# Hybrid attention and expert block: where the experts' collected rows are summed, gated and added

## The chip, the cores and the metric

The kernel runs on one core of one Trainium2 chip. The time is the device time of one launch in microseconds; lower is better. Engines are called as the profile calls them: PE (matmuls), PEld (its weight loads), DVE (VectorE), ACT (ScalarE), POOL (GpSimd) and SP (SyncE, which here only issues DMAs). Each engine works through its own list of instructions in order, so an instruction that waits holds up all that stand behind it on that engine.

## The reference

Two layers run over 256 latent tokens and 256 context tokens of width 1024, in float32. A layer is a modulated norm, a projection, two branches (neighbourhood attention, and a long convolution), a gated merge into `x`, and then a mixture of 32 experts of which every token takes two. The last layer computes only the latent tokens to the end; of the context it needs keys and values.

```python
def _layer(x, xc, c, c_ctx, last, ...):
    h = _rms(x, norm_mix) * (1.0 + sc1) + sh1          # hc for the context in the same way
    q, k, v, hy, gates = _project(h, w_in, q_norm, k_norm)
    ...
    x = x + g1 * _merge(attn, hyena, gates, w_br_a, w_br_b, w_out)
    h2 = _rms(x, norm_ffn) * (1.0 + sc2) + sh2
    x = x + g2 * _hier_moe(h2, ...)                    # top-1 group, two experts of it
    if last:
        return x, xc
    ...
    xc = xc + g2c * _hier_moe(h2c, ...)
    return x, xc
```

An expert computes `(silu(h2 @ w1) * (h2 @ w3) * weight) @ w2`; a token's two results are added, multiplied by the gate `g2` (one row of 1024 for the latent tokens, another for the context) and added to `x`.

## The kernel before, in words

Rows of tokens are held in tiles of 128: in layer one tiles 0 and 1 are latent and 2 and 3 context (`nt` is 4, `full` is true), in layer two there are only 0 and 1. `xm[0]` holds rows 0 and 1 side by side, `xm[1]` rows 2 and 3.

The expert stage (`moe`, `first_round`) goes through eight groups `q` of four experts, two pairs of experts each; below, pair p is experts 2p and 2p+1, so group 6 is pairs 12 and 13 and group 7 is pairs 14 and 15. Of each expert three blocks of 1 MiB are loaded by SP (`fetch`, line 1391) into a ring of SBUF buffers: two for the first product, one for the second. A block is loaded as soon as the block that had its buffer has been used. For a pair PE runs the first product (`w13`, L1411, 32 matmuls), `hidden` makes the gate product out of it (ACT `sl`, DVE `hd` at L1365, two transposes at L1368, ACT `hdT`), and PE runs the second product (`w2`, L1426, 16 matmuls). The second product of a pair waits for its gate product; the first product of the next pair stands around it.

Groups 0 to 5 write their results to DRAM, in rows by token (`scatter`, L1292, into `ybuf`, two rows for a token). Groups 6 and 7 don't: their results stay in SBUF and are brought to the tokens' rows by matmuls with a one-hot matrix (`add`, L1456), and `residual` multiplies by the gate and adds to `x`. What groups 0 to 5 wrote is read back by `collect(i)`: POOL issues two loads of 512 KiB for row tile i (L1306), and the `add` that it returns sums them, multiplies by `g2` and adds to `x`: three DVE instructions over 128x1024 for each of the tiles, all on DVE. In layer one `collect(0)` and `collect(1)` are called in group 6, `collect(2)` and `collect(3)` in group 7 after the first gate product; in layer two `collect(0)` in group 6 and `collect(1)` in group 7. `collect(0)` also loads `g2` (L394, SP). In layer one rows 0 and 2 go to the buffer s21, all others to the two rotating buffers `t4`.

The code's order is not the order of the engines' lists. A planner sorts the instructions by its own estimates of times: an instruction goes on its engine's list when, by the estimate, its inputs are there. It can so put an instruction that waits for a DMA ahead of one that comes before it in the code. `issue_after(ins)` forbids that for one instruction: what is inside stands behind `ins` on the same engine's list, and that is all it does.

After group 7 a block that runs only when an expert has over 64 tokens is passed by a branch (L1350); nothing moves across it. Layer two begins with `head([0, 1])`: norm (`xn`, L457), transposes (L461), scaled and split to `hT`. The projection that follows runs 12 times 24 matmuls (`proj_T`, L239 to L241), each with a weight tile `wsp` that ACT and DVE split in advance; `head([2, 3])` for the context stands after the sixth of them. It calls `residual(i, half, None)`, which adds what groups 6 and 7 gave the context's rows (kept in `rest`, buffer s21) to `x`. Layer two's expert ring has 16 buffers, s15 among them.

## Time and profile before

| what | value |
|---|---|
| time, median of 3 runs | 1447.03 us (1446.01 to 1447.13) |
| profiled execution | 1441.07 us |
| its span | 1439.3 us |
| PE busy | 1281.0 us (89%) |
| DVE busy | 660.3 us (46%) |
| ACT busy | 455.8 us (32%) |
| POOL busy | 211.0 us (15%) |
| moved by DMA | 373.04 MB, mean 259 GB/s |
| expert stage of layer one | about 603 to 885 us |
| expert stage of layer two | about 1180 us to the end |

The profile is one execution. Its times count from the span's start. In the timeline a row gives the start, the time taken, the engine, the line, the operation, what it writes and reads, and in brackets how long the engine had been idle before it and whose end released it. A span's busy share does not tell what bounds a stage; that is read from the waits of the stage.

### The profile page before, as it was taken

What the parts mean: (1) busy time and instruction counts of PE and PEld (TensorE: products, weight loads), DVE (VectorE), ACT (ScalarE), POOL (GpSimd) and SP (SyncE); (2) the same over time, 40 slices, a digit from 0 to 9 for tenths busy, and PEclk for the clock granted to TensorE, in tenths of its full rate; (3) what the DMA queues carried; (4) which work ended last, traced back from release to release, by engine and by line L of the source; (5) the groups of instructions that cost most, each with busy time, mean ns of one, the idle gap of its engine ahead of it and who ended that gap; (6) DMA issues with size and microseconds to landing.
All of it is one profiled execution on the core that took longest, in us unless ns stands there. A gap on an engine that the chain in (4) does not pass through costs nothing. (4 is left out here: it accounts for less than half of the span.)

```text
span 1439.3 us, 18183 instructions
## 1 busy us (share of the span) xinstructions
PE 1281.0 (89%) x7071; PEld 831.1 (58%) x7071; DVE 660.3 (46%) x1361; ACT 455.8 (32%) x884; POOL 211.0 (15%) x175
## 2 busy tenths in 40 slices
PE   5999999999999999599888397999899969998776
PEld 2555777886578887344333134899779943443222
DVE  4654366676677666601000137865774760100014
ACT  3433223337632133222211014533574522221101
POOL 2021033361000000211110000032500021110000
PEclk9999999999999999699999699999999979999989
DMA  9744625455177762799999963325326749999991
GB/s 377 282 166 185 230 90 190 159 219 215 59 262 274 288 241 98 278 408 420 419 420 422 403 274 137 129 106 211 136 94 219 259 161 380 418 419 420 422 407 69
DMA packets 65691, 373.04 MB, mean 259 GB/s; under 512 B 11994, under 2 KB 13338, under 8 KB 26048
## 3 DMA queue, kind: packets, MB, share of 16 engines
q1 hardware_dynamic: 54368, 347.67, 61.9%
q0 software_dynamic: 10368, 21.02, 4.1%
q10 hardware_dynamic: 864, 3.15, 0.5%
q8 instruction: 57, 0.93, 0.3%
q14 instruction: 34, 0.28, 0.1%
HBM read 362.06 MB, written 27.53 MB: 271 GB/s over the span
## 5 line engine op out<-in xcount | busy, mean ns | idle before, releaser
L1411 PE MATMUL pW<-we,xT 128*64 128x512 f32 x1024 | 263.0, 605 | 8.5 <-DMA we<-in_wexp_dram 8.4
L1411 PEld LDWEIGHTS pW<-we,xT 128*64 128x64 f32 x1024 | 82.3, 138 | 149.8 <-issue 131.7
L239 PE MATMUL pA<-hT,wsp 128*128 128x512 f32 (+1 forms) x448 | 156.3, 349 | 4.0 <-ACT hf L223 4.0
L1365 DVE SCALAR_TENSOR_TENSOR hd<-sl,cws,pW 128x256 f32<-128x256 f32 x32 | 15.3, 480 | 305.9 <-ACT sl L223 305.9
L241 PE MATMUL pA<-hT,wsp 128*128 128x512 f32 (+1 forms) x448 | 154.4, 345 | 1.1 <-DVE wsp L220 1.1
L240 PE MATMUL pA<-hT,wsp 128*128 128x512 f32 (+1 forms) x448 | 154.0, 344 | 0.0
L220 DVE TENSOR_TENSOR wsp<-win,wsp 128x1024 fp32r<-128x1024 f32 x80 | 102.1, 1281 | 105.8 <-ACT wsp L223 105.6
L1426 PE MATMUL pW<-we,hdT 128*64 128x512 f32 x512 | 142.0, 621 | 4.9 <-ACT hdT L223 4.7
L223 ACT ACTIVATE wsp<-win 128x1024 fp32r<-128x1024 f32 x80 | 84.1, 1057 | 141.9 <-PE pA L241 137.2
L240 PE MATMUL pA<-wsp,hT 128*128 128x256 f32 x352 | 99.9, 284 | 2.6 <-DVE wsp L220 2.6
L239 PE MATMUL pA<-wsp,hT 128*128 128x256 f32 x352 | 100.2, 285 | 0.7 <-ACT vv L223 0.7
L241 PE MATMUL pA<-wsp,hT 128*128 128x256 f32 x352 | 99.7, 283 | 0.0
L239 PEld LDWEIGHTS pA<-hT,wsp 128*128 128x128 f32 x448 | 86.2, 192 | 21.6 <-issue 8.0
L240 PEld LDWEIGHTS pA<-hT,wsp 128*128 128x128 f32 x448 | 86.1, 192 | 13.7 <-issue 6.1
L241 PEld LDWEIGHTS pA<-hT,wsp 128*128 128x128 f32 x448 | 85.9, 192 | 11.1 <-issue 1.8
L1426 PEld LDWEIGHTS pW<-we,hdT 128*64 128x64 f32 x512 | 48.6, 141 | 73.3 <-issue 59.2
L223 ACT ACTIVATE Y<-pW 128x512 f32<-128x512 f32 (+1 forms) x64 | 38.2, 597 | 137.0 <-PE pW L1426 134.7
L223 ACT ACTIVATE sl<-pW 128x256 f32<-128x256 f32 x32 | 12.3, 383 | 218.7 <-PE pW L1411 218.7
L248 POOL TENSOR_TENSOR rs<-rsq,mh 128x1 f32<-128x1 f32 x14 | 8.4, 601 | 424.9 <-DVE rsq L247 414.0
L239 PEld LDWEIGHTS pA<-wsp,hT 128*128 128x128 f32 x352 | 67.3, 191 | 5.3 <-issue 2.5
L240 PEld LDWEIGHTS pA<-wsp,hT 128*128 128x128 f32 x352 | 67.4, 191 | 3.4 <-DVE wsp L220 3.2
L241 PEld LDWEIGHTS pA<-wsp,hT 128*128 128x128 f32 x352 | 67.4, 191 | 0.2
(301 smaller groups left out, 2324.4 us busy)
## 6 DMA issues: line engine op xcount, KB each, us to landing
we<-in_wexp_dram SPq DMA_DIRECT2D x190, 1024.0 KB
win<-in_win_dram SPq DMA_DIRECT2D x40, 1024.0 KB
ada<-in_ada_dram SPq DMA_DIRECT2D x32, 1024.0 KB
ada<-in_adaj_dram SPq DMA_DIRECT2D x16, 1024.0 KB
wbr<-in_wbr_dram SPq DMA_DIRECT2D x8, 1024.0 KB
wout<-in_wout_dram SPq DMA_DIRECT2D x8, 1024.0 KB
ybuf<-zero SPq DMA_DIRECT2D x12, 512.0 KB
bc<-modd SPq DMA_DIRECT2D x12, 512.0 KB
```

Source lines behind the costliest of these rows:

```text
L220: (eng or self.nc.vector).tensor_tensor(out=out, in0=a, in1=b, op=op)
L223: self.nc.scalar.activation(out, in_, func, **kw)
L239: self.nc.tensor.matmul(out, lh, rh, start=start, stop=False)
L240: self.nc.tensor.matmul(out, lh, rl, start=False, stop=False)
L241: self.nc.tensor.matmul(out, ll, rh, start=False, stop=stop)
L248: nc.gpsimd.tensor_tensor(out=out, in0=t, in1=self.mh[:, : shape[1]], op=ALU.pow)
L1365: nc.vector.scalar_tensor_tensor(out=hd, in0=sl, scalar=cws, in1=pa[:, 256:512], op0=ALU.mult, op1=ALU.mult)
L1411: nc.tensor.matmul(pa[64 * e : 64 * e + 64, :], xT[:, kc, cs], wt[(2 * p + e, kc // 4)][:, kc % 4, :], start=kc == 0, stop=kc == KC - 1)
L1426: nc.tensor.matmul(py[64 * e : 64 * e + 64, :], hdT[:, fc, 64 * e : 64 * e + 64], wt[(2 * p + e, 2)][:, fc, hs], start=fc == 0, stop=fc == 1)
```

## The change

The sum and the gate product move from DVE to POOL for all rows, and the two row tiles of latent tokens are collected together in group 6 in both layers; in layer two the first of them gets the buffer s15, for which the expert ring gives that buffer up for its last 16 blocks. What is left on DVE for the latent tokens is one addition to `x` for each tile, ordered behind the last gate product (`last_hd`, pair 15). The context's rows of layer one are no longer collected in the expert stage: their four loads, and one of the context's gate row (`gc`, SP), stand behind the branch; POOL sums and gates them in the head of layer two, and DVE adds them to `x` in `head([2, 3])`, ahead of `residual`.

```diff
--- before.py
+++ after.py
@@ -443,6 +443,7 @@
             i0, n = tiles[0], len(tiles)
             for i in tiles:
                 if not full and i > 1:
+                    self.tt(xs[1][:, i % 2, :], xs[1][:, i % 2, :], self.crows[i - 2][0], ALU.add)
                     for half in range(2):
                         self.residual(i, half, None)
                 x_ = xs[i // 2][:, i % 2, :]
@@ -473,6 +474,13 @@
             head([0, 1, 2, 3])
         else:
             head([0, 1])
+            y0, y1, gc = self.crows[0]
+            first = nc.gpsimd.tensor_tensor(out=y0, in0=y0, in1=y1, op=ALU.add).ins
+            with self.tc.issue_after(first):
+                self.tt(y0, y0, gc, ALU.mult, nc.gpsimd)
+                y0, y1, gc = self.crows[1]
+                self.tt(y0, y0, y1, ALU.add, nc.gpsimd)
+                self.tt(y0, y0, gc, ALU.mult, nc.gpsimd)
         if full:
             self.filter(0, 0, (17, 19), 12, "B", "B", "C")
             self.ft = self.fin[2]
@@ -1297,19 +1305,19 @@
             nonlocal g2
             if i == 0:
                 g2 = self.bcast(l, 3, 0 if full else 20, ns)
-            if full and i % 2 == 0:
-                yr = self.S(21, [P, 2, D], name="yr")
+                yr = self.S(21 if full else 15, [P, 2, D], name="yr")
                 yt = [yr[:, 0, :], yr[:, 1, :]]
             else:
                 yt = [self.T4([P, D], name="yt") for _ in range(2)]
             for k in range(2):
                 nc.gpsimd.dma_start(yt[k], ybuf[(k * nt + i) * P : (k * nt + i) * P + P, :])
+            self.tt(yt[0], yt[0], yt[1], ALU.add, nc.gpsimd)
+            self.tt(yt[0], yt[0], g2[:, 0, :], ALU.mult, nc.gpsimd)
 
             def add():
-                x_ = xm[i // 2][:, i % 2, :]
-                self.tt(yt[0], yt[0], yt[1], ALU.add)
-                self.tt(yt[0], yt[0], g2[:, i // 2, :], ALU.mult)
-                self.tt(x_, x_, yt[0], ALU.add)
+                x_ = xm[0][:, i, :]
+                with self.tc.issue_after(self.last_hd):
+                    self.tt(x_, x_, yt[0], ALU.add)
             return add
 
         ssn = [self.st([P, 2], "ss", 4) for _ in range(nt if full else 0)]
@@ -1355,6 +1363,16 @@
                     nc.sync.dma_start(self.out[0, i * P : i * P + P, hs], xm[0][:, i, hs])
         self.xres, self.rsn = xm, rsn
         self.residual = residual
+        if full:
+
+            gc = self.T4([P, D], name="gc")
+            nc.sync.dma_start(gc, self.modd[l, 3, 1:2, :].partition_broadcast(P)[:, 0, :])
+            self.crows = []
+            for i in (2, 3):
+                yr = self.S((17, 19)[i - 2], [P, 2, D], name="yc")
+                for k in range(2):
+                    nc.gpsimd.dma_start(yr[:, k, :], ybuf[(k * nt + i) * P : (k * nt + i) * P + P, :])
+                self.crows.append((yr[:, 0, :], yr[:, 1, :], gc))
 
     def hidden(self, pa, cws):
 
@@ -1362,7 +1380,8 @@
         sl = self.TH([P, 256], name="sl")
         self.act(sl, pa[:, 0:256], AF.Silu)
         hd = self.TH([P, 256], name="hd")
-        nc.vector.scalar_tensor_tensor(out=hd, in0=sl, scalar=cws, in1=pa[:, 256:512], op0=ALU.mult, op1=ALU.mult)
+        self.last_hd = nc.vector.scalar_tensor_tensor(out=hd, in0=sl, scalar=cws, in1=pa[:, 256:512],
+                                                      op0=ALU.mult, op1=ALU.mult).ins
         ptt = self.ps("X", [P, 2, P])
         for fc in range(2):
             nc.tensor.transpose(ptt[:, fc, :], hd[:, fc * P : fc * P + P], self.ident)
@@ -1385,7 +1404,8 @@
         else:
             order = [(e, k) for e in range(NEXP) for k in range(3)]
             order[84:] = [(e, k) for e in range(28, 32) for k in range(2)] + [(e, 2) for e in range(28, 32)]
-            seq = [15, 18, 11, 13, 16, 21, 2, 3, 17, 19, 4, 5, 6, 7, 8, 9] * 6
+            seq = [15, 18, 11, 13, 16, 21, 2, 3, 17, 19, 4, 5, 6, 7, 8, 9] * 5
+            seq += seq[1:16] + [18]
         prev = [max([-1] + [m for m in range(n) if seq[m] == seq[n]]) for n in range(96)]
 
         def fetch():
@@ -1478,16 +1498,13 @@
                 spread(q)
             hdT = self.hidden(w13(2 * q, z["xT"], fill), z["cw"][:, 0:1])
             if q == 7:
-                for u in adds:
-                    u()
-                adds = [collect(i) for i in range(nt // 2, nt)]
                 self.banks["X"] = [7]
             if q > 5:
                 z["Y"].append(self.S(ys[0][q % 2], [P, 2, D], F32R, name="Y"))
                 outs.append(to_parts(z["Y"][0]))
             fill = w2(2 * q, hdT, outs[0])
             if q == 6:
-                adds = [collect(i) for i in range(nt // 2)]
+                adds = [collect(i) for i in range(2)]
             if q == 7:
                 fill += [lambda x=x: open_(*x) for x in units]
             hdT = self.hidden(w13(2 * q + 1, z["xT"], fill), z["cw"][:, 1:2])
```

## Rows read from the trace of the kernel before

**Rows 1.** The page: its first line, and PE's share of the span.
```profile
span 1439.3 us, 18183 instructions
...
PE 1281.0 (89%) x7071; PEld 831.1 (58%) x7071; DVE 660.3 (46%) x1361; ACT 455.8 (32%) x884; POOL 211.0 (15%) x175
```
**Rows 2.** PE's waits, 600 to 880 us: total us, times, longest us.
```profile
PE pX L1368 <- DVE hd L1365: 31.2, 7, 22.8
```
**Rows 3.** PE's waits, 1180 us to the end.
```profile
PE pX L1368 <- DVE hd L1365: 17.8, 5, 13.8
```
**Rows 4.** Timeline around pair 12's gate product, layer one.
```profile
790.17 0.38 ACT L223 ACTIVATE sl<-pW 128x256 f32<-128x256 f32 x1 [6.55 <-PE pW L1411]
...
792.63 1.07 POOL L1306 DMA_DIRECT2D yt<-ybuf  x2
...
811.30 1.23 DVE L220 TENSOR_TENSOR yt<-yt,yt 128x1024 f32<-128x1024 f32 x1 [6.29 <-DMA yt<-ybuf]
812.44 0.48 DVE L1365 SCALAR_TENSOR_TENSOR hd<-sl,cws,pW 128x256 f32<-128x256 f32 x1
...
812.97 0.69 PE L1368 MATMUL pX<-cst,hd 128*128 128x128 f32 x2 [22.84 <-DVE hd L1365]
```
**Rows 5.** Timeline around pair 12's gate product, layer two.
```profile
1362.33 0.38 ACT L223 ACTIVATE sl<-pW 128x256 f32<-128x256 f32 x1 [7.95 <-PE pW L1411]
1374.43 1.23 DVE L220 TENSOR_TENSOR yt<-yt,yt 128x1024 f32<-128x1024 f32 x1 [26.72 <-DMA yt<-ybuf]
1375.57 0.48 DVE L1365 SCALAR_TENSOR_TENSOR hd<-sl,cws,pW 128x256 f32<-128x256 f32 x1
...
1376.11 0.69 PE L1368 MATMUL pX<-cst,hd 128*128 128x128 f32 x2 [13.81 <-DVE hd L1365]
```
**Rows 6.** Both stretches by windows: busy by engine, then PEclk, DMA share, GB/s.
```profile
790.00:813.00 23.00, 0.16 (x2) 0.03 (x1) 2.84 (x3) 0.38 (x1) 2.39 (x5) 0.60 1.01 418
...
1362.00:1376.00 14.00, 0.29 (x1) 0.00 (x0) 1.57 (x2) 0.38 (x1) 1.21 (x3) 0.59 1.02 421
```
**Rows 7.** Timeline, pair 15 of layer one.
```profile
864.60 0.38 ACT L223 ACTIVATE sl<-pW 128x256 f32<-128x256 f32 x1 [9.98 <-PE pW L1411]
...
867.42 0.47 DVE L1365 SCALAR_TENSOR_TENSOR hd<-sl,cws,pW 128x256 f32<-128x256 f32 x1
...
868.86 5.37 PE L1426 MATMUL pW<-we,hdT 128*64 128x512 f32 x16 [0.47 <-ACT hdT L223]
```
**Rows 8.** Windows where the weights' stream ends, both layers.
```profile
844.00:846.00 2.00, 2.00 (x12) 0.64 (x10) 0.00 (x0) 0.00 (x0) 0.00 (x0) 1.00 0.04 16
846.00:848.00 2.00, 2.00 (x10) 0.56 (x6) 0.00 (x0) 0.00 (x0) 0.00 (x0) 1.00 0.00 0
...
1410.00:1412.00 2.00, 2.00 (x10) 0.63 (x10) 1.79 (x2) 0.35 (x1) 0.00 (x0) 1.00 0.05 19
```
**Rows 9.** Timeline, PE in pairs 14 and 15 of layer two.
```profile
1401.42 7.08 PE L1411 MATMUL pW<-we,xT 128*64 128x512 f32 x30
...
1423.50 3.65 PE L1426 MATMUL pW<-we,hdT 128*64 128x512 f32 x16
```
**Rows 10.** Timeline, PE in the head of layer two: first projection, context's transposes.
```profile
893.28 0.51 PE L239 MATMUL pA<-hT,wsp 128*128 128x256 f32 x1 [2.57 <-ACT hf L223]
...
913.35 0.60 PE L461 MATMUL pA<-cst,xn 128*128 128x128 f32 x4
```
**Rows 11.** Timeline, collecting row tile 2 in layer one.
```profile
853.01 1.05 POOL L1306 DMA_DIRECT2D yr<-ybuf  x2 [39.66 <-DVE x L220]
...
860.36 1.22 DVE L220 TENSOR_TENSOR yr<-yr 128x1024 f32<-128x1024 f32 x1 [5.02 <-DMA yr<-ybuf]
```
**Rows 12.** Groups of POOL by form: count | busy us, mean ns | idle before.
```profile
L220 POOL TENSOR_TENSOR Yj<-Yj,t 128x512 f32<-128x512 f32 x24 | 32.3, 1357 | 141.6 <-DVE t L220 121.4 <-ACT hf L223 20.2
...
L220 POOL TENSOR_TENSOR wf<-Yj 128x512 f32<-128x512 f32 x12 | 20.9, 1740 | 0.9
```
**Rows 13.** Timeline, SP in layer two's projection: issues and the waits between them.
```profile
907.07 32.19 SPq L212 DMA_DIRECT2D win<-in_win_dram  x5
```

## The prediction

> **What bounds the kernel now.** I read the page first, then PE's waits in each of the two expert stages, then the timeline around the longest wait, then the windows of the stretch with the DMA share, and last the place where the weights' stream ends. PE is busy for 1281.0 us of the span of 1439.3 us [rows 1], so what can be won is idle time of PE at places where PE is last.
>
> PE's longest single waits in both expert stages are of one kind: the transposes of a gate product wait for DVE's `hd`, once for 22.8 us in layer one [rows 2] and once for 13.8 us in layer two [rows 3]. The timeline shows why. In layer one ACT has pair 12's `sl` at 790.17 + 0.38 = 790.55 us, but `hd` starts at 812.44, because the planner put the sum of the collected rows `yt` ahead of it, and that sum starts only at 811.30, when its load has landed. The load was issued at 792.63 [rows 4]. In layer two `sl` is there at 1362.71, the sum starts at 1374.43, `hd` at 1375.57 [rows 5]. During both waits the DMA engines are full, 418 and 421 GB/s [rows 6]: the collected rows come late because the weights' stream fills the same engines, and while PE waits the stream runs ahead of it. PE's granted clock falls to a mean of 0.60 and 0.59 there, which lies between full speed and the low level of 1.2 GHz, so PE also starts again slowly.
>
> The gain has a second limit. The stream of weights cannot end earlier merely because DVE no longer waits. In layer one packets still move in the window 844 to 846 us and none in the next; in layer two a few still move between 1410 and 1412 us [rows 8]. The last product of a layer needs the last blocks.
>
> **Part 1: the sums and gates of the latent rows leave DVE (layer one).** `hd` of pair 12 can start at about 790.6 instead of 812.44, 21.9 us earlier. At pair 15 six DVE instructions for the context's rows stand ahead of `hd` too: `sl` is there at 864.98, `hd` starts at 867.42, 2.4 us late [rows 7]. Both go. By PE alone the second product of pair 15, which starts at 868.86 [rows 7], would start 21.9 + 2.4 = 24.3 us earlier, at 844.6. By the stream it can start when the last block is in, at about 846 [rows 8]. The later one counts: 846, a gain of 22.9 us. That product took 5.37 us against 3.65 us for the same 16 matmuls in layer two [rows 7, 9]; if PE comes to it at full clock another 1.7 us fall away, if PE has idled for the last blocks they don't. I take 23 us; the bounds are 18 (both products of pair 15 at the low clock, some 5 us) and 28 (the stream ends earlier, and PE alone counts: 24.3 + 1.7, and some 2 us of low clock behind the wait that go too).
>
> **Part 2: the same in layer two.** `hd` of pair 12 starts at about 1362.75 instead of 1375.57, 12.8 us earlier. By PE alone the last second product starts at 1423.50 - 12.8 = 1410.7 [rows 9]. The stream gets 0.5 MiB more ahead of its end (the second load of row tile 1 now goes with the other three), 0.52 MB at 421 GB/s or 1.25 us, so it ends at about 1412.5 instead of 1411.3 [rows 6, 8]. The blocks on the way also hold PE, which works in order. An estimate from these rows: 9.5 MiB stand behind the first block of expert 29 in the stream, 2.5 us each, so that block lands at 1412.5 - 23.7 = 1388.8. Behind it PE has half of pair 13's second product (half of 3.65), some ten one-hot products (7.08 / 30 = 0.24 us each), 7.1 for pair 14's first product, and the 15.0 us that lie between the end of that product and the start of the last one, 1408.50 to 1423.50 [rows 9]: 1388.8 + 1.8 + 2.4 + 7.1 + 15.0 = 1415.1. So the product starts at 1412.5 to 1415 and the gain is 8.4 to 11; I take 9.5, with bounds of 4 (low clock after a wait, as in part 1) and 13 (PE alone).
>
> **Part 3: what comes to POOL.** Eight instructions over 128x1024 in layer one, four in layer two. No row has that size; POOL took 1.36 and 1.74 us for 128x512 [rows 12], so I estimate 2.7 to 3.5 us each, against 1.22 us on DVE [rows 11]. The latent ones are hidden: the rows are in at 811 and 1374, the four instructions take 14 us at most, plus a wait for the gate row, and DVE needs them only behind the last gate product, which comes some 1 to 2 us ahead of the last second product, at about 845 and 1412. If that cover were gone, DVE would hold pair 15's results up by what is missing. What is left for DVE there is two additions of 1.22 us, in the time in which pair 15's second product runs (3.65 us): nothing. Behind POOL's waiting instructions on its own queue stands nothing that is due in the expert stages.
>
> **Part 4: the context's rows in the head of layer two.** Times here are on the clock of before. The loads can start behind the branch, at about 886.5 us; four issues at some 0.55 us, and landing about 7.4 us after the first issue of a tile, as in layer one once the stream is over [rows 11]. So POOL starts at about 894 and has four instructions of 2.7 to 3.5 us: the second tile is ready at 905 to 908. Addition to `x`, `residual`, norm: another 6 us, 911 to 914. PE comes to the context's transposes at 913.35 [rows 10]. So PE waits for 0 to 1 us by this, up to 4 if the gate row lands late; if the planner sets DVE's additions early, DVE stands for some us, which the weight tiles split in advance cover. DVE also gets rid of eight instructions in the expert stage and keeps four. I take a loss of 1 us, bounds -1 and 5.
>
> The trace shows that POOL's time for one shape lies between 1.36 and 1.74 us, the longer one where DVE works between two SBUF tiles beside it [rows 12]. The Trainium skill ("SBUF — State Buffer", section "Who interferes with whom") says more: a DVE instruction with two SBUF inputs and a POOL instruction that reads SBUF exclude each other for the whole instruction. By that rule four POOL instructions of some 3 us in the head could hold DVE's splits for up to 12 us, and the sum would come out about 5 us higher than mine. The spread of the rows agrees with some interference; no row shows DVE blocked for a whole POOL instruction.
>
> The ring of layer two loses one buffer of 16 for its last 16 blocks, and the last of them waits for pair 13's second product instead of its first. By part 2 that product is done at about 1388.8 + 1.8 = 1390.6, and the block should land at 1412.5: there are 20 us between, so nothing.
>
> **The sum.** 23 + 9.5 - 1 = 31.5 us off the profiled execution of 1441.07 us: 1409.6 us. That execution lies 6.0 us under the median of 1447.03, so the median should be 1415.5 us.
>
> **The rivals.**
> *A, the stream ends sooner.* If the few engines that finish last catch up because the ring is kept free, only PE's order counts: 28 + 13 = 41 us, 1406 us. For it: the share in 844 to 846 is only 0.04. Against: no stretch of the wait was without a full stream, and the bytes are the same.
> *B, half of it is given back.* PE now waits for blocks in pairs 13 to 15, the clock falls as in rows 6, and the last products run at the rate of rows 7; 5 us less in each layer and 4 more in the head: 17.5 us gained, 1429.5 us. For it: PE at the end of layer one was slow after a wait of only some 3 us. Against: the stream's waits are spread, 1 to 5 us each.
> *C, slower than before.* The context's gate row `gc` is issued by SP, and SP's list in the head holds loads that wait for buffers: five of them took 32.19 us [rows 13]. If the planner puts `gc` behind these, it lands at about 945 instead of 892 (on the clock of before); POOL's two gate products, the norm and the transposes follow, PE stands at the context's transposes from 913 to about 957, 44 us, and the result is 12 us over before, 1459 us. It decides the sign when `gc` lands later than about 934 (934 + 12 - 913 = 33). Against: `gc` is the first load behind the branch in the code, and its buffer is free once the latent residual is done.
> *D, it doesn't do what it says.* `hd` of pair 12 still stands behind something that waits for a DMA, because only the additions are ordered and nothing else: 1447 us. Against: no other DVE instruction of that stretch reads what a DMA of POOL brings.
>
> **How the numbers follow.** Forecast 0.60, A 0.08, B 0.20, C 0.07, D 0.05. The forecast's own range is 24 to 37 us gained, 1410 to 1423. With most of A and B the range is 1405 to 1434. What can be told from no change is 0.2%, 2.9 us. Faster: forecast, A and B, 0.88; within it: D, 0.05; slower: C, 0.07.
>
> **What would show it.** In PE's waits of both expert stages the entries of 22.8 and 13.8 us for `hd` must be gone, and waits for weight blocks of 1 to 5 us each must stand in their place; pair 15's second product should start at about 846 in layer one, and PE's list from there to the first projection should keep its 24.4 us or so [rows 7, 10]. In layer two the distance from pair 12's gate product to the span's end, 63.7 us now, should grow to about 67, since the first comes 12.8 us earlier and the second 9.5. POOL's twelve instructions should take 2.7 to 3.5 us each. Wrong would be: a wait of over 5 us at the context's transposes or at `hd` of pair 15, an end of the stream in layer one before 840 us, or products of pair 15 at twice their usual time.

## The result and the profile after

The changed kernel takes 1423.93 us (median of 4 runs, 1420.83 to 1427.82) against 1446.52 us for the kernel before on the same chip (4 runs, 1443.29 to 1447.13). The ratio is 0.985, with a 95% interval of 0.9818 to 0.9881. So it is 22.6 us faster, where 31.5 were forecast. The time is inside the whole range of 1405 to 1434 us, 0.9 us outside the forecast's own of 1410 to 1423, and the gain is 9 us short. The profiled execution took 1420.83 us against 1441.07, so its 20.2 us are what the traces can account for.

The page of the changed kernel, its first line and the busy shares (answering to [rows 1]). POOL has 12 instructions and 29.5 us more, DVE 12 instructions and 12.5 us less, and PE is as busy as before in a shorter span:

```profile
span 1419.1 us, 18192 instructions
...
PE 1281.9 (90%) x7071; PEld 833.5 (59%) x7071; DVE 647.8 (46%) x1349; ACT 456.6 (32%) x884; POOL 240.5 (17%) x187
```

PE's waits in the expert stage of layer one (answering to [rows 2]; total us, times, longest us). The wait of 22.8 us for `hd` is gone, the longest is now 1.0. The waits for weight blocks, of which the kernel before had three as well (third line), have grown from 2.9 to 4.3 us:

```profile
PE pX L1387 <- DVE hd L1383: 7.0, 7, 1.0
PE pW L1431 <- DMA we<-in_wexp_dram: 4.3, 3, 2.7
PE pW L1411 <- DMA we<-in_wexp_dram: 2.9, 3, 1.6
```

The same in layer two (answering to [rows 3]). The 13.8 us are gone too, and three waits for blocks, 5.5 us in all in the kernel before (third line), have become five with 9.2 us, the longest 3.4 us in both:

```profile
PE pW L1431 <- DMA we<-in_wexp_dram: 9.2, 5, 3.4
PE pX L1387 <- DVE hd L1383: 5.9, 6, 1.0
PE pW L1411 <- DMA we<-in_wexp_dram: 5.5, 3, 3.4
```

The timeline around pair 12's gate product in layer one (answering to [rows 4]). `hd` follows `sl` by 0.04 us, the loads of the collected rows are issued beside it, and PE waits 0.99 us instead of 22.84:

```profile
788.98 0.38 ACT L223 ACTIVATE sl<-pW 128x256 f32<-128x256 f32 x1 [7.15 <-PE pW L1431]
789.40 0.48 DVE L1383 SCALAR_TENSOR_TENSOR hd<-sl,cws,pW 128x256 f32<-128x256 f32 x1 [15.62 <-ACT sl L223]
789.61 1.17 POOL L1313 DMA_DIRECT2D yr<-ybuf  x2 [7.02 <-DMA ybuf<-Y,gi]
...
789.94 0.44 PE L1387 MATMUL pX<-cst,hd 128*128 128x128 f32 x2 [0.99 <-DVE hd L1383]
```

Windows of the two stretches (answering to [rows 6]): the clock stays at 0.97 and 0.91, where it had fallen to 0.60 and 0.59, and the DMA engines are as full as before:

```profile
790.00:805.00 15.00, 11.74 (x44) 4.24 (x46) 1.38 (x2) 1.58 (x3) 4.15 (x5) 0.97 1.02 421
1353.00:1373.00 20.00, 15.71 (x58) 5.81 (x58) 1.86 (x3) 1.96 (x4) 4.96 (x5) 0.91 1.02 419
```

PE at the end of layer one and at the first projection of layer two (answering to [rows 7, 10]): the last second product starts at 844.69 and takes 3.70 us instead of 5.37, and the first projection starts at 866.39 instead of 893.28:

```profile
844.69 3.70 PE L1446 MATMUL pW<-we,hdT 128*64 128x512 f32 x16 [0.47 <-ACT hdT L223]
...
866.39 0.39 PE L239 MATMUL pA<-hT,wsp 128*128 128x256 f32 x1 [1.15 <-ACT hf L223]
```

So far the change does what was foreseen. The time is lost right behind. PE's waits from 855 to 970 us in the changed kernel have an entry that the kernel before has not (there the same wait is 0.5 us):

```profile
PE pA L521 <- DVE u L545: 10.7, 2, 9.8
```

DVE's list at that place. `u` is what PE waits for. Between its two instructions stands the addition of context tile 2's collected rows, which waits 7.68 us for POOL and takes 3.35 us instead of 1.22; the next split of a weight tile is behind it:

```profile
870.16 0.48 DVE L543 SCALAR_TENSOR_TENSOR u<-pA,prm,u 128x255 f32<-128x255 f32 x1 [1.25 <-ACT u L223]
878.33 3.35 DVE L220 TENSOR_TENSOR x<-x,yc 128x1024 f32<-128x1024 f32 x1 [7.68 <-POOL yc L220]
881.60 0.47 DVE L545 SCALAR_TENSOR_TENSOR u<-pA,prm,u 128x255 f32<-128x255 f32 x1
881.99 1.21 DVE L220 TENSOR_TENSOR wsp<-win,wsp 128x1024 fp32r<-128x1024 f32 x1
```

PE's own list shows what it stood at. After the matmuls of two projection tiles come the transposes of the first tile's `u`; the third tile's matmuls follow them at once, so its weight tile had been split:

```profile
882.21 0.68 PE L521 MATMUL pA<-cst,u 128*128 128x128 f32 x2 [9.82 <-DVE u L545]
882.54 0.56 PE L239 MATMUL pA<-hT,wsp 128*128 128x256 f32 x1
```

And POOL: the loads of tile 2 are issued at 861.49 behind the branch, are in at 871.34, and then both sums stand ahead of both gates, so tile 2's rows are ready with the first gate, at 878.3. DVE's addition starts there and ends 1.1 us behind the second gate, which ends at 880.6:

```profile
861.49 1.16 POOL L1374 DMA_DIRECT2D yc<-ybuf  x2 [1.88 <-DVE xn L458]
...
871.34 2.36 POOL L478 TENSOR_TENSOR yc<-yc 128x1024 f32<-128x1024 f32 x1 [8.17 <-DMA yc<-ybuf]
873.66 2.33 POOL L220 TENSOR_TENSOR yc<-yc 128x1024 f32<-128x1024 f32 x1
875.96 4.63 POOL L220 TENSOR_TENSOR yc<-yc,gc 128x1024 f32<-128x1024 f32 x2
```

Windows around it: PE is busy for 1.79 of the 8 us from 876, the clock is at 0.50 (the lower of its two levels), and in the next 8 us, with PE full, still 0.88:

```profile
876.00:884.00 8.00, 1.79 (x9) 1.82 (x10) 5.53 (x5) 1.08 (x2) 5.13 (x3) 0.50 0.23 66
884.00:892.00 8.00, 8.00 (x61) 8.00 (x61) 6.38 (x12) 4.42 (x9) 0.00 (x0) 0.88 0.09 11
```

To compare all executions I cut the trace at four instructions that every kernel has, counted in PE's list: the 401st matmul of the experts' first products (the middle of pair 12's in layer one), the first projection of layer two, the first expert matmul of layer two, and PE's last instruction. The stretches are in us, each from one profiled execution:

| | A: pair 12 to first projection | H: first projection to layer two's first expert matmul | D: from there to PE's end |
|---|---|---|---|
| before | 107.1 | 287.2 | 249.4 |
| changed | 82.0 | 302.9 | 240.9 |
| difference | -25.1 | +15.7 | -8.5 |

These make -17.9; the stretch ahead of A was 1.8 us shorter in this execution, although nothing is changed there, and what lies behind PE's last instruction is 0.5 us shorter. Together these are the 20.2 us. Over all the profiled executions below, the stretch ahead of A differs by up to 6.0 us (784.4 to 790.4), with nothing changed in it. H leaves this out, so it tells the kernels apart more sharply than the whole time does.

Windows of H and D, before and after in turn (the first number behind the length is PE's busy time). H has 13.3 us more of waits and 2.3 us more of busy time; D has 8.9 us less of waits and the same busy time:

```profile
893.28:1180.54 287.26, 264.81 (x1922) 238.80 (x1922) 197.73 (x430) 136.10 (x262) 48.93 (x34) 0.96 0.46 164
866.39:1169.30 302.91, 267.14 (x1922) 240.28 (x1922) 204.30 (x435) 138.06 (x267) 60.15 (x39) 0.94 0.46 166
1180.54:1429.92 249.38, 218.61 (x996) 87.53 (x994) 27.94 (x74) 48.25 (x96) 26.37 (x28) 0.95 0.89 362
1169.30:1410.15 240.85, 218.94 (x998) 88.05 (x995) 23.14 (x70) 48.23 (x96) 35.70 (x32) 0.97 0.92 375
```

### The profile page after: what moved, and what is told of

Read it like the earlier page. It is cut to its first block, busy times and chain, and to the rows that moved or that the text cites. A ratio compares the mean times of both kernels' runs of the same rounds, so it can differ in the third digit from the quotient of the medians.

```text
span 1419.1 us, 18192 instructions
## 1 busy us (share of the span) xinstructions
PE 1281.9 (90%) x7071; PEld 833.5 (59%) x7071; DVE 647.8 (46%) x1349; ACT 456.6 (32%) x884; POOL 240.5 (17%) x187
## 5 line engine op out<-in xcount | busy, mean ns | idle before, releaser
L1431 PE MATMUL pW<-we,xT 128*64 128x512 f32 x1024 | 265.9, 611 | 13.9 <-DMA we<-in_wexp_dram 13.5
L1446 PE MATMUL pW<-we,hdT 128*64 128x512 f32 x512 | 136.4, 598 | 5.1 <-ACT hdT L223 4.7
L240 PEld LDWEIGHTS pA<-hT,wsp 128*128 128x128 f32 x448 | 86.1, 192 | 13.8 <-issue 6.1
L223 ACT ACTIVATE sl<-pW 128x256 f32<-128x256 f32 x32 | 12.3, 383 | 227.2 <-PE pW L1431 227.2
```

Source lines behind the costliest of these rows:

```text
L223: self.nc.scalar.activation(out, in_, func, **kw)
L240: self.nc.tensor.matmul(out, lh, rl, start=False, stop=False)
L1431: nc.tensor.matmul(pa[64 * e : 64 * e + 64, :], xT[:, kc, cs], wt[(2 * p + e, kc // 4)][:, kc % 4, :], start=kc == 0, stop=kc == KC - 1)
L1446: nc.tensor.matmul(py[64 * e : 64 * e + 64, :], hdT[:, fc, 64 * e : 64 * e + 64], wt[(2 * p + e, 2)][:, fc, hs], start=fc == 0, stop=fc == 1)
```

## The experiments

The first four kernels ask what makes the loss in H. The theory was DVE standing in its list order for rows that POOL has not ready; the rival for some of the runs was that place or origin of the rows does not matter.

**e1: the two additions later in DVE's list.** They are put behind the last `u` of the fourth projection tile:

```diff
-                    self.tt(xs[1][:, i % 2, :], xs[1][:, i % 2, :], self.crows[i - 2][0], ALU.add)
+                    with self.tc.issue_after(self.uls[3]):
+                        self.tt(xs[1][:, i % 2, :], xs[1][:, i % 2, :], self.crows[i - 2][0], ALU.add)
```
(`uls` holds the second `scalar_tensor_tensor` of each projection tile.)

> The changed kernel, with DVE's two additions of the context's collected rows ordered behind the second u instruction of the fourth projection tile; POOL and the DMAs do the same as before. Theory (the list): the changed kernel loses some 15 us in the head of layer two because the first addition stands on DVE's list ahead of the u that PE's next transposes need, and waits there for POOL. Then PE's longest wait for u (9.8 us) falls under 2 us and the time comes to 1409 to 1415 us. Rival (contention): POOL's instructions and the four loads themselves slow DVE and PE in the head, wherever the addition stands: 1420 to 1425 us, as the changed kernel (1423.9).

Measured: 1416.38 us (1413.18 to 1419.38), ratio to before 0.9798 (0.9776 to 0.9819). H is 294.7, so about half of the 15.7 us came back, less than expected. The wait for `u` is 1.1 us, but PE now waits 4.1 us at the context's transposes, since the norm starts later. And DVE is slow while POOL works. POOL's chain takes 12.5 us instead of 9.3, and DVE's splits beside it 1.83 to 2.21 us instead of 1.22:

```profile
876.92 2.41 POOL L479 TENSOR_TENSOR yc<-yc 128x1024 f32<-128x1024 f32 x1 [7.93 <-DMA yc<-ybuf]
879.29 3.40 POOL L220 TENSOR_TENSOR yc<-yc 128x1024 f32<-128x1024 f32 x1
882.66 6.74 POOL L220 TENSOR_TENSOR yc<-yc,gc 128x1024 f32<-128x1024 f32 x2
```

DVE at the same time in e1:

```profile
878.59 1.83 DVE L220 TENSOR_TENSOR wsp<-win,wsp 128x1024 fp32r<-128x1024 f32 x1
...
881.74 2.03 DVE L220 TENSOR_TENSOR wsp<-win,wsp 128x1024 fp32r<-128x1024 f32 x1
...
884.91 2.21 DVE L220 TENSOR_TENSOR wsp<-win,wsp 128x1024 fp32r<-128x1024 f32 x1
```

**e2: the context's rows left out.** Their loads, POOL's four instructions and DVE's two additions are removed, so the context tiles lack what groups 0 to 5 of experts gave them.

> The changed kernel without the collected rows of the context: their loads, POOL's four instructions and DVE's two additions are left out, so the context lacks what groups 0 to 5 gave it. Theory (the list): all of the loss in the head comes from that chain; the head takes what it took before, and the time is 1406 to 1411 us. Rival (the head loses for another reason, such as the weights' loads that arrive later behind the stream): 1418 us or more.

Measured: 1414.21 us (1410.63 to 1416.2), ratio 0.9782 (0.9762 to 0.9802). That is between the two, 3.2 us over the theory's upper end and 3.8 under the rival's lower one, and 9.7 us under the changed kernel. H is 290.4: without the rows it is still 3.2 us over before.

**e3: the context part alone.** The kernel before, with only the context's rows moved to layer two's head; the latent rows stay on DVE as they were.

> The kernel before, with only the context's rows moved to the head of layer two (loads behind the branch, POOL's four instructions, DVE's additions in the head); the latent rows are summed, gated and added as before. Theory (the list): this part alone is a loss: the waits of 22.8 and 13.8 us for hd stay, 2.4 us at pair 15 go, some 13 to 15 us are lost in the head: 1456 to 1460 us. Rival (the head loses only because the expert stage now ends while the stream still fills the DMA engines): nothing is lost there, 1443 to 1447 us.

Measured: 1455.22 us (1454.46 to 1457.46), ratio 1.0073 (1.0056 to 1.009): 9.6 us slower than before, 0.8 us under the theory's range. H is 302.9, the same to 0.1 us as in the changed kernel, and the wait for `u` is again 9.8 us. Stretch A is 4.9 us shorter (102.2), for DVE has less to do there, and D is 249.4 as before. So this part by itself is a loss, and the latent rows' part makes D's 8.5 us and the other 20.2 of A's 25.1.

**e4: the two context buffers exchanged.** Tile 2 goes into the buffer whose loads stand ahead of the branch:

```diff
-                yr = self.S((17, 19)[i - 2], [P, 2, D], name="yc")
+                yr = self.S((19, 17)[i - 2], [P, 2, D], name="yc")
```

> The changed kernel with the two buffers of the context's rows swapped, so that the row tile that is added first has the buffer that comes free first. Its loads are then issued at about 843 us instead of 861, and POOL can sum it at once; its gate waits only for gc. Theory (the list): the first addition is ready at about 870 to 872 us instead of 878, PE's wait for u falls from 9.8 us to 2 to 5, and the time is 1413 to 1419 us. Rival (contention): POOL and the loads do the same amount of work, 1420 to 1425 us.

Measured: 1419.32 us (1417.12 to 1420.97), ratio 0.9816 (0.98 to 0.9832), 0.3 us over the theory's upper end and 0.7 under the rival's range. H falls to 297.0, but A rises to 86.0: POOL's first sum now runs at 855 us, in the tail of layer one, and PE waits 3.0 us instead of 0.9 for DVE's `xg` there. POOL's first gate, which now has its rows early, waits 3.29 us for the gate row `gc`.

The next four vary the place, the order and the engine.

**e5: e1 and e4 together.** The edit is the sum of the two.

> The late additions of e1 (behind the fourth projection tile's last u) together with the swapped buffers of e4 (context tile 2 in the buffer that is free early). Theory: in e1 the wait for Pool is gone already, so data that come earlier bring nothing, while Pool's first sum, now at about 855 us in the tail of layer one, holds DVE there for some us, as in e4, where the stretch from weight pass 400 to the first projection took 86.0 us against 82.3 in e1. Theory: 1418 to 1421, 2 to 4 us above e1. Rival, the rows' arrival is what e1 still loses by: 1411 to 1414. Sign: the first projection's distance from weight pass 400 (theory 85 to 87 us, rival 82 to 83).

Measured: 1418.67 us (1417.02 to 1422.48), ratio 0.982 (0.9797 to 0.9843). The theory held: A is 85.1, and H (292.9) gives back no more than A lost.

**e6: as e1, with the sums and gates on DVE.** POOL does none of the rows' arithmetic (against the changed kernel; its four instructions on POOL are taken out, and `uls` is as in e1):

```diff
-                    self.tt(xs[1][:, i % 2, :], xs[1][:, i % 2, :], self.crows[i - 2][0], ALU.add)
+                    with self.tc.issue_after(self.uls[3]):
+                        y0, y1, gc = self.crows[i - 2]
+                        self.tt(y0, y0, y1, ALU.add)
+                        self.tt(y0, y0, gc, ALU.mult)
+                        self.tt(xs[1][:, i % 2, :], xs[1][:, i % 2, :], y0, ALU.add)
```

> As e1, but the two sums and the two gates of the context's rows are done by DVE, in front of its additions, and Pool does none of the rows' arithmetic in the head of layer two. Theory (DVE and Pool shut each other out while both read SBUF): DVE gets four instructions of 1.22 us more (4.9 us), and its weight-tile splits beside them, 1.8 to 2.2 us in e1, are back at 1.2, the additions too (1.7 to 1.2): 0.6 + 0.8 + 1.0 + 1.0 us returned, so e1 plus 1 to 2 us, 1416 to 1419. Rival (the splits are stretched by the transfers of that time, not by Pool): they stay at 1.8 to 2.2 us and the sum is e1 plus 5 or more, 1421 to 1424.

Measured: 1420.17 us (1414.33 to 1422.72), ratio 0.9831 (0.9812 to 0.9849); H is 297.4. With POOL silent all of DVE's instructions of this size, the rows' own and the splits among them, take 1.21 to 1.23 us (the first row is two):

```profile
880.65 2.35 DVE L220 TENSOR_TENSOR yc<-yc 128x1024 f32<-128x1024 f32 x2
...
885.18 1.21 DVE L220 TENSOR_TENSOR x<-x,yc 128x1024 f32<-128x1024 f32 x1
886.32 1.22 DVE L220 TENSOR_TENSOR wsp<-win,wsp 128x1024 fp32r<-128x1024 f32 x1
```

So it is POOL, and not the transfers, that stretches DVE's instructions. The time is over what the theory gave all the same, 3.8 us above e1 instead of 1 to 2. DVE is full in this stretch, and PE waits 11.9 us for `xn` instead of some 7 (for `xn` and `rsq` together) in e1. Whether four instructions more on DVE cost more than POOL's interference is not clear of noise: the intervals of e6 and e1 overlap, and H is only 1.0 to 2.7 us over the two profiles of e1's kernel (e1, e11).

**e7: additions two tiles earlier, and POOL tile by tile.** The additions stand behind `uls[1]`, and POOL's order is sum and gate of tile 2, then sum and gate of tile 3.

> The additions held only until the second projection tile's last u (two tiles earlier than e1), and Pool's rows in another order: sum and gate of tile 2, then sum and gate of tile 3. Theory (what is left of e1's loss is that the context's norm starts late: PE waits 4.1 us at the context's transposes for a chain that begins with the additions): tile 2 is ready some 4.7 us earlier, DVE stands for Pool under 1 us, the 4.1 us wait falls under 1 us, and the time is 1409 to 1413. Rival (DVE is full in this stretch whatever the order): the wait moves to other tiles and the time is 1415 to 1418.

Measured: 1418.03 us (1416.76 to 1419.25), ratio 0.9812 (0.9795 to 0.9829); H is 297.3. The theory fell, the rival held, at its upper end: the wait at the transposes is down to 1.6 us, and a wait of 5.9 us for `u` has come back. DVE does not stand idle for POOL at all in this kernel. It loses the time inside its instructions: four of 1.22 us take 3.41, 2.30, 3.39 and 2.63, which is 6.9 us too much:

```profile
873.67 3.41 DVE L220 TENSOR_TENSOR wsp<-win,wsp 128x1024 fp32r<-128x1024 f32 x1
...
878.12 2.30 DVE L220 TENSOR_TENSOR wsp<-win,wsp 128x1024 fp32r<-128x1024 f32 x1
880.34 3.39 DVE L220 TENSOR_TENSOR x<-x,yc 128x1024 f32<-128x1024 f32 x1
...
884.38 2.63 DVE L220 TENSOR_TENSOR wsp<-win,wsp 128x1024 fp32r<-128x1024 f32 x1
```

**e8: additions behind `uls[1]`, POOL's order unchanged.**

> As e1, but the additions held only until the second projection tile's last u, two tiles earlier; Pool's order as in the changed kernel (both sums, then both gates). Theory: DVE now stands some 1 to 3 us for Pool's gate of tile 2, which ends at about 886 us, while PE still has split weight tiles to work on; the context's norm comes about 5 us earlier than in e1: 1411 to 1415. Rival (any place in front of the last projection tile makes DVE stand and PE with it): 1418 to 1422, near the changed kernel.

Measured: 1418.75 us (1415.76 to 1419.74), ratio 0.981 (0.9789 to 0.983), the rival's number. DVE stands 4.62 us for POOL, and PE waits 7.4 us for `u`. Two tiles of `u` decide between 1.1 us of wait (e1; 2.9 in e11) and 7.4.

After these the theory was shaken: every kernel with POOL's four instructions in the head had H at 293 to 303, whatever the order. The last kernels were to take the wait and the four instructions apart.

**e9: the additions no longer read POOL's rows.** The additions read a tile of `x` that has long been there. The result of POOL's work is not used, so the context tiles are given wrong rows:

```diff
-                    self.tt(xs[1][:, i % 2, :], xs[1][:, i % 2, :], self.crows[i - 2][0], ALU.add)
+                    self.tt(xs[1][:, i % 2, :], xs[1][:, i % 2, :], xs[0][:, i % 2, :], ALU.add)
```

> The changed kernel with DVE's two additions in the head of layer two reading a tile of x that is long in place instead of the context's collected rows; the loads, Pool's two sums and two gates stay and their result is not used (the context tiles get wrong rows). So DVE has the same two instructions, and nothing of it waits for Pool. Theory (DVE's stand for Pool, with the tiles queued behind it, is most of the head's loss of 15.7 us): head and norm run as in before apart from what Pool shuts out, 1412 to 1416. Rival (the exclusion by Pool's four instructions is most of it): 1418 to 1422. From first projection to the first expert product: theory 290 to 294 us, rival 297 to 301 (before 287.2, changed kernel 302.9, without the rows 290.4).

Measured: 1422.38 us (1419.21 to 1424.37), ratio 0.9836 (0.9818 to 0.9854); H is 300.2. The theory's numbers are missed; H lies in the rival's range, and the time 0.4 us above it. But the experiment did not take the wait away. The planner, which found the additions' inputs in place, set them earlier in DVE's list (they run at 866.27 and 870.55), and the trace shows another wait behind them: the context's norm needs `rs`, a product over 128x1 that POOL makes, and in POOL's queue it now stands behind the four instructions, until 884.77:

```profile
874.22 2.62 POOL L478 TENSOR_TENSOR yc<-yc 128x1024 f32<-128x1024 f32 x1 [8.15 <-DMA yc<-ybuf]
876.81 2.82 POOL L220 TENSOR_TENSOR yc<-yc 128x1024 f32<-128x1024 f32 x1
879.60 4.63 POOL L220 TENSOR_TENSOR yc<-yc,gc 128x1024 f32<-128x1024 f32 x2
...
884.77 0.57 POOL L248 TENSOR_TENSOR rs<-rsq,mh 128x1 f32<-128x1 f32 x1
```

DVE in e9: `xn` waits 7.59 us for it, again between the two halves of the first `u`, and the small addition ahead takes 2.82 us instead of 0.68:

```profile
874.58 2.82 DVE L220 TENSOR_TENSOR x<-x,rest 128x512 f32<-128x512 f32 x1
877.32 0.47 DVE L543 SCALAR_TENSOR_TENSOR u<-pA,prm,u 128x255 f32<-128x255 f32 x1
885.38 0.75 DVE L458 TENSOR_SCALAR xn<-x,rs 128x1024 f32<-128x1024 f32 x1 [7.59 <-POOL rs L248]
```

**e10: e9 without POOL's four instructions.** The loads stay, and DVE's list is that of e9, instruction by instruction.

> As e9, and Pool's two sums and two gates of the context's rows are left out as well; the loads stay. DVE's list is the same as in e9, instruction by instruction. The difference between the two is the price of Pool's four instructions by themselves. Theory: Pool holds DVE for about as long as each of its instructions meets a two-input DVE instruction, some 3 to 6 us in all, of which PE sees half: e10 is 2 to 3 us under e9, and DVE's splits of 128x1024 all take 1.2 us, in e9 some of them 2 us and more. Rival (Pool's instructions cost nothing of PE's time once nothing waits for them): equal within 1 us. Absolute: 1411 to 1414.

Measured: 1412.34 us (1412.06 to 1416.47), ratio 0.9775 (0.9757 to 0.9792); H is 289.7. The difference to e9, with the same work on all other engines, is 10.0 us, where 2 to 3 were expected. In e10 POOL has `rs` at 875.09, and DVE does not wait for it:

```profile
875.09 0.93 POOL L248 TENSOR_TENSOR rs<-rsq,mh 128x1 f32<-128x1 f32 x1 [8.02 <-DVE rsq L247]
```

As DVE's lists are equal, the two traces can be laid side by side. The small addition that POOL stretches by 2.14 us in e9 costs nothing there: in e10 DVE waits 2.47 us for ACT right behind it, in e9 not at all. DVE falls behind when `xn` waits its 7.59 us, and once more when PE comes back slowly from its own wait (from 889 to 897 us its clock is 0.80 in e9 and 1.00 in e10, and DVE waits 2.38 us for ACT's `u` instead of 0.12). So most of the 10.0 us is again DVE standing for POOL: the rival's number came out by the theory's mechanism.

**e11 and e12: e1 and the changed kernel again, side by side on one chip.**

> The kernel of e1 again, beside the changed kernel on one chip and with five rounds, since it is the fastest that keeps the whole computation and its interval touches that of the changed kernel. Theory (7 to 8 us of the head's loss come from the place of the additions in DVE's list): 1415 to 1419 and 5 to 8 us under the changed kernel. Rival (the first result was the spread of the runs): within 3 us of the changed kernel.

> The changed kernel as it is, on the same chip as e9 to e11, as their measure: 1421 to 1425 by the first result. If it comes out under 1419, the place of the additions is worth less than the single profiles say.

Measured: 1414.89 us (1413.72 to 1418.67), ratio 0.9791 (0.9774 to 0.9808), and 1423.23 us (1421.36 to 1425.54), ratio 0.9847 (0.9832 to 0.9862). The intervals lie apart: e1 is 8.3 us under the changed kernel, with the whole computation, and the rival of a mere spread is out (both numbers of the theory are met to 0.3 us). It has the lowest median of the kernels that keep the computation, and it lies 2.6 us over e10, which has none of the rows' arithmetic on POOL in the head; these two intervals overlap. H was 296.4 and 302.0 here against 294.7 and 302.9 the first time, so a single profile tells H to some 2 us. By H the price of the best place is higher: e1's kernel lies 5.0 and 6.7 us over e10, the changed kernel 12.3 and 13.2.

## Why the prediction was right or wrong

**Part 1 was right about the wait, wrong about the limit, and 2 us small.** The last second product of layer one starts at 844.69, and this execution ran 1.8 us ahead of the one before at the start of A; on the clock of before that is 846.5, and 846 was named, with the end of the stream as its limit. That limit did not hold it: behind one wait of 2.70 us at 804.53 PE waits for no weight block in layer one any more, and the last second product waits 0.47 us for `hdT` alone. So the time came from PE's own order, for which 844.6 had been worked out without that wait, and that 846 was met is in part luck. I took the product at its old 5.37 us, and it took 3.70. From its start to the first projection it is 21.7 us instead of 24.4. So stretch A gave 25.1 us where I took 23; the bounds of 18 to 28 hold it.

**Part 2 was right.** 9.5 us were named, D gave 8.5. From pair 12's gate product in layer two (1352.34) to the span's end (1419.1) are 66.8 us; about 67 were named. The waits for blocks have grown as was looked for, though not from nothing: from three with 5.5 us to five with 9.2.

**Part 3 was right about the cover in the expert stages.** The row additions wait for nothing there. None of POOL's eight instructions there meets a DVE instruction that it stretches. The size was high: POOL takes 2.33 to 2.36 us for 128x1024 when it is alone, not 2.7 to 3.5. Beside DVE it takes up to 3.5.

**Part 4 is the step that failed.** I took a loss of 1 us with bounds of -1 and 5; H lost 15.7. The end of the chain was right, but by two errors that cancel: on the clock of before tile 3's rows were to be ready at 905 to 908, which is 878 to 881 after the 26.9 us by which the head comes earlier, and POOL ended at 880.6. It began at 871.34, which is 898.2 on the clock of before and 4.2 us later than the 894 that were taken, and took 9.3 us instead of 11 to 14. The gate row's load, rival C's price, was issued at 861.00 and held nobody. What was wrong is the overlap, in one sentence: "if the planner sets DVE's additions early, DVE stands for some us, which the weight tiles split in advance cover". The trace of before showed both halves nearly. DVE's list in its head shows where the planner puts the context's additions, and PE's shows how much work it has before it needs `u`:

```profile
889.12 0.68 DVE L220 TENSOR_TENSOR x<-x,rest 128x512 f32<-128x512 f32 x1
...
898.55 0.48 DVE L535 SCALAR_TENSOR_TENSOR u<-pA,prm,u 128x255 f32<-128x255 f32 x1 [0.94 <-ACT u L223]
...
900.63 0.40 PE L513 MATMUL pA<-cst,u 128*128 128x128 f32 x2
```

The additions of `rest`, ahead of which the new one must stand, run from 889.12, ahead of the first `u`. Three weight tiles are split by the first projection (two from 876.84 us, one from 887.78), but PE can use only two of them: the transposes of the first tile's `u` stand in its list behind 48 matmuls and ahead of the third tile. So what covers a wait of DVE there is 48 matmuls, 893.28 to 900.63, and not the split tiles. The first addition needs tile 2's rows, three POOL instructions behind 894: by the prediction's own numbers 902 to 904.5. With the addition and the rest of `u` (1.22 and 0.47 us) that leaves some 3 to 6 us of PE's time open. In the changed kernel PE ran the 48 matmuls from 866.39 to 872.4 and waited for 9.8 us; the rows came at 878.33, which is 905.2 on the clock of before.

Of H's 15.7 us, 10.2 are the wait for `u` (10.7 us against 0.5), 2.3 are PE's longer busy time, where the clock was low behind that wait, and 2.8 are new waits at the context's transposes (`xn` and `rsq`: 5.1 us in all against 2.3, which are the latent tiles'). The rest is in small waits of either sign.

**My own theory of the loss, DVE's wait for the late rows, holds for the larger part of it and not for all.** e8 and e9 show the wait: DVE stands 4.6 and 7.6 us for something of POOL's, once for the rows and once for a small product behind them in POOL's queue, and e9 against e10 shows that such a stand is paid in full. e7 shows a price without any standing: 6.9 us inside four DVE instructions, and H 7.6 us over e10's. In the changed kernel `u` is held up by 7.68 us of standing and by an addition that takes 3.35 us, 2.13 too much; so there the standing is about four fifths of what is too much. Against e10 the changed kernel loses 10.9 us (1423.23 - 1412.34), and e1, the best place found, 2.6. How far the loss would fall if only one of the two were taken away no kernel here shows, since in every kernel with less of the one there was more of the other.

DVE and POOL shut each other out here for whole instructions. In e7 a split of 1.22 us takes 3.41 beside POOL's 2.39, and in e6, where POOL is silent, all take 1.21 to 1.23. In e1 the times can be worked out from each other: POOL's second sum ends 2.27 us behind the split that ends at 880.42, as it would if it had started there (2.33 us alone), and the split that starts at 881.74 ends 1.08 us behind that sum; the next split and POOL's last gate, worked out in the same way, agree to 0.2 us. `u`, which reads its first input from PSUM (`pA`), keeps its 0.47 to 0.48 us beside them. The Trainium skill ("SBUF — State Buffer", section "SBUF: two separate sides") says that of a DVE instruction with two SBUF inputs and a POOL instruction that reads SBUF the one that starts first has the ports they share for its whole length, and that the other is blocked. The traces here agree with the page. The prediction named this at 5 us over its sum, 1420.5 us for the time, and gave it no chance; that this number is nearer than its own is luck, for in the changed kernel the exclusion stretches one instruction, by 2.13 us. The prediction's reason, that no row shows DVE blocked for a whole POOL instruction, holds for the rows that it quotes. The trace of before has such a row, an instruction that takes 0.69 us elsewhere:

```profile
944.67 1.29 POOL L220 TENSOR_TENSOR wf<-Yj 128x512 f32<-128x512 f32 x1
944.72 1.79 DVE L220 TENSOR_TENSOR wf<-Yj 128x512 f32<-128x512 f32 x1
```

**The rivals.** By number the result lies nearer to B (17.5 us) than to the forecast, but B's mechanism did not occur: the last second products took 3.70 and 3.65 us, and the clock stood at 0.97 and 0.91. A's number was not reached, C's gate row came in time, and D's `hd` stands behind no DMA. None of the signs of being wrong would have caught the loss: PE stood at `u`, which they do not name, and at the context's transposes for no more than 1.7 us at once.

**Against the forecast of 31.5 us off** there are 25.1 + 8.5 - 15.7 = 17.9 us in the three stretches of the profile, and 22.6 by the medians. The parts for the expert stages were 1.1 us better than forecast together, the head 14.7 worse. Of the 4.7 us between these two, 1.8 lie ahead of A and 0.5 behind PE's last instruction; the other 2.4 are what the medians differ by more than the two profiled executions.

**What stays open.** H without POOL's four instructions is 2.5 to 3.2 us over before (e10, e2), little more than a single profile can tell. In several executions PE waits once 2.1 us for DVE's `c` late in the projections, followed by some us at a lower clock, and in others it doesn't. The same kernel shows both (e1 without, e11 with), so it does not come from the lists alone; what decides it was not tried.

## What to carry to other kernels

Work that goes to an idle engine isn't free where the receiver is an engine with an ordered list: look up where in that list the receiving instruction will stand, what stands behind it, and for how long the engine that bounds the stage has work in hand by its own list, up to the first instruction that needs the receiver. Here the trace of before showed the last two, and by the additions of `rest` about where the first would be. And a POOL instruction that reads SBUF is to be put where DVE is idle, as in the expert stages, where eight of them stretched nothing and nothing waited for them; in a stretch where DVE is full, four of them cost 2.6 us in the best place (5.0 to 6.7 by H) and 10.9 us (12.3 to 13.2 by H) in the one that the planner chose.

## What the hardware showed that was not expected

- An addition on DVE over 128x1024 that takes 1.22 us took 3.34 to 3.39 us beside a POOL instruction on SBUF (changed kernel, e7, e8), and one over 128x512 2.82 us instead of 0.68 (e9). POOL's instruction is stretched too, from 2.33 to 3.4 us (e1).
- POOL needs 2.33 us for 128x1024 by itself, less than twice the 1.36 us that its rows for 128x512 showed [rows 12].
- An instruction with one input can be shut out as well: in e4 a cast of 128x256 on DVE took 2.10 us instead of 0.29 beside a POOL instruction of 2.38 us.
- In layer two the wait of 13.8 us went and PE's waits for weight blocks grew from 5.5 to 9.2 us. D became 8.5 us shorter by waits alone: PE's busy time in it is 218.61 us before and 218.94 after.
